# A hybrid encoder trunk: the delta net's first loads, norms and products in a written order on TensorE, VectorE and ScalarE

## The chip, the cores and the metric

One Trainium2 chip, one of its cores. The metric is the device time of one execution in microseconds, the median of several runs. TensorE is PE, VectorE is DVE, ScalarE is ACT, GpSimd is POOL; SP is the engine that issues most DMAs. All data are float32; matrix products run in float32r on a high and a low part of each operand.

## What is computed

A trunk of two layers over 1024 positions of width 1024: a gated delta net, and chunked attention over shared keys and values, each followed by a gated convolution FFN, with RMS norms between. The part that the change touches is the beginning of the delta net:

```python
h = x
xn = rmsnorm(h, a_norm[0])              # x * rsqrt(mean(x*x) + EPS) * g
proj = xn @ a_w_in[0]                   # 1024 x (4096 + 16)
qkv = silu(causal_dwconv(proj[..., :3072], a_conv[0]))   # four taps
z = proj[..., 3072:4096]
b_raw, a_raw = proj[..., 4096:4104], proj[..., 4104:4112]
beta = sigmoid(b_raw)
g = -exp(A_log) * softplus(a_raw + dt_bias)
```

## The kernel before, in words

Activations are kept transposed: 8 tiles of 128 channels, each in two halves `s` of 512 positions. Each is split into a rounded high part `xh[k][s]` (made by ACT, line 1100) and the rest `xl[k][s]` (made by DVE, line 1101); a weight tile of 1024 x 128 is split the same way into `whi` (a cast on ACT, line 103) and `wlo` (POOL, line 105). One product of an output tile is eight units of three PE instructions (`dense`, lines 120 to 122): high by high, high by low, low by high.

The start is `begin_input`. `take_x` issues the load of 128 rows of x (512 KB) on SP's queue. `norm_x` squares and sums a tile on ACT, takes the root, and DVE divides: reciprocal, then one multiply over the whole tile. `turn_x(s)` transposes four such tiles, 128 columns at a time, into a PSUM bank (`pxt`, three banks in turn), from which ACT and DVE make `xh` and `xl` with the norm's gain `g_a`. The first two weight tiles (keys of heads 0 and 1, columns 8 and 9 of 128) are loaded and split at once by `load_w`. Then for each half `s` and each of the two tiles come eight units of products, with one further step of `turn_x` after each unit as long as there is one. `post(s, ps)`, made by `project`, empties the tile's PSUM bank through the four taps of the short convolution (`taps`, DVE) and a silu (tanh on ACT, two operations on POOL). `load_gates`, `project_gates` and `gates` do the 16 columns of beta and the decay.

`colt` (all per-channel constants, 128 x 489, among them `g_a`, the taps `ca`, the FFN's taps) and `rowt` (16 numbers, broadcast to 128 partitions) are loaded at the very top by ACT's own DMA queue; `ca` is halved by DVE soon after.

In the begin PE's order is as written (a manual schedule of PE alone); DVE, ACT and POOL are ordered by the scheduler. Behind the begin a planner, `Flow`, deals out the rest of the delta net by modelled times and writes out the order of PE, DVE and ACT. During the begin it runs in a mode (`auto`) in which `later` calls a step at once.

Of the kernel before, what the change touches and what calls it, by code (L numbers as in the profile page):

```python
# [16 lines left out]
P = 128  # L17
# [11 lines left out]
def trunk_kernel(  # L29
# [22 lines left out]

    ncol = cols.shape[1]
    colt = const.tile([P, ncol], F32, name="colt")
    nc.scalar.dma_start(out=colt, in_=cols)
    o = 0
    def take(n):
        nonlocal o
# [8 lines left out]
    g_b = take(8)  # L67
    g_o = take(1)
    rowt = const.tile([P, 16], F32, name="rowt")
    nc.scalar.dma_start(out=rowt, in_=rows[:, 0:16].broadcast_to([P, 16]))  # L70
    alog = rowt[:, 0:8]
    dtb = rowt[:, 8:16]

# [126 lines left out]
    class Flow(Weave):  # L200
# [4 lines left out]
        def __init__(self):  # L205
            super().__init__()
            self.T, self.free, self.aux = 0.0, dict(D=0.0, A=0.0, G=0.0), deque([[0.0], [0.0]])
            self.time, self.items, self.last, self.stalls = {}, [], 0, []
            self.auto, self.tick, self.slack, self.cur, self.nxt, self.units = True, 0, 0.5, None, deque(), 0
            self.brief, self.early, self.split_at, self.hold = False, 8, 8, None  # L210

        def mark(self, key, t=None):
            super().mark(key)
# [37 lines left out]
            return self.aux[-1]  # L251

        def full(self, rank):
            return rank >= 2 and max(self.free["D"], self.free["A"]) - self.T > 4.0

        def pick(self):
            if self.dense and self.dense[0][0]():
# [252 lines left out]
    with ExitStack() as ph:  # L510
# [11 lines left out]
        nc.vector.tensor_reduce(upper, ident.rearrange("p (b h j) -> p h b j", b=4, h=2)[:, 0], axis=AX.XY, op=ALU.add)  # L522
        early_dp = ExitStack()
        dq = early_dp.enter_context(tc.tile_pool(name="dq", bufs=1, side="right", **SB))

        nc.vector.tensor_scalar(ca, ca, 0.5, None, op0=ALU.mult)

        ba = dp.tile([P, 8, 16], F32, name="ba")

# [539 lines left out]
        def gate_z(hd):  # L1069
            def post(s, ps):  # L1070
                zt = dp.tile([P, HALF], F32, name="zt", tag="zt", bufs=3)
                nc.scalar.copy(zt, ps)
                nc.sync.dma_start(out=d_z[hd][s], in_=zt)
                wv.mark(("z", hd, s), wv.on("A", 0.6) + 3.0)

            return 3072 + hd * P, post
# [6 lines left out]
            x_tiles.append(t_.rearrange("p j t -> p (j t)")[:, 0:SEQ])  # L1083
            nc.sync.dma_start(out=x_tiles[i], in_=x[i * P : (i + 1) * P, :])

        def norm_x(i):
            t_ = x_tiles[i]
            jk = dp.tile([P, 8, P], F32, name="xj", tag="U", bufs=2).rearrange("p c t -> p (c t)")
            r = dp.tile([P, 2], F32, name="rsx", tag="rsx", bufs=4)
            nc.scalar.activation(jk, t_, AF.Square, accum_out=r[:, 0:1])  # L1090
            nc.scalar.activation(r[:, 1:2], r[:, 0:1], AF.Sqrt, scale=1.0 / SEQ, bias=epst)
            nc.vector.reciprocal(r[:, 1:2], r[:, 1:2])
            nc.vector.tensor_scalar(t_, t_, r[:, 1:2], None, op0=ALU.mult)

        def turn_x(s):
            for k in range(KT):
                ps = (pone if k % 3 == 2 else paux).tile([P, HALF], F32, name="pxt", tag="pm" if k % 3 == 2 else "pa")
                for t in range(4):
                    nc.tensor.transpose(ps[:, t * P : (t + 1) * P], x_tiles[4 * s + t][:, k * P : (k + 1) * P], ident)
                nc.scalar.activation(xh[k][s], ps, AF.Copy, scale=g_a[:, k : k + 1])  # L1100
                nc.vector.scalar_tensor_tensor(xl[k][s], ps, g_a[:, k : k + 1], xh[k][s].bitcast(F32), op0=ALU.mult, op1=ALU.subtract)  # L1101
                yield

        def load_gates():
            raw = dp.tile([P, KT, 16], F32, name="raw16", tag="at", bufs=4)
            w16 = dp.tile([P, KT, 32], F32R, name="w16", tag="ke", bufs=4)
            nc.sync.dma_start(out=raw, in_=a_w_in[:, 4096:4112].rearrange("(k p) m -> p k m", p=P))
            nc.scalar.copy(w16[:, :, 0:16], raw)
            nc.gpsimd.tensor_tensor(w16[:, :, 16:32], raw, w16[:, :, 0:16].bitcast(F32), op=ALU.subtract)
            gT = [dq.tile([32, HALF], F32, name="gT", tag="mn", bufs=8) for _ in range(2)]  # L1110
            return w16, gT

        def project_gates(w16, gT, s):
# [49 lines left out]
        def begin_input():  # L1163

            warm = dp.tile([P, 2], F32, name="warm", tag="rsx", bufs=4)
            nc.scalar.activation(warm[:, 0:1], epst, AF.Sqrt)
            for i in range(4):
                take_x(i)
            for i in range(4):
                norm_x(i)  # L1170
            wts = [load_w(a_w_in, m * P) for m in (8, 9)]
            for i in range(4, 8):
                take_x(i)
            for s in range(2):
                if s == 1:
                    for i in range(4, 8):
                        norm_x(i)
                it = turn_x(s)
                for _ in range(3):
                    next(it)  # L1180
                for n, (wt, post) in enumerate(zip(wts, posts)):
                    ps = pacc.tile([P, HALF], F32, name="acc", tag="acc", bufs=3)
                    for i in range(KT):
                        dense(ps, wt, 0, xh, xl, FULL[i : i + 1], s, first=i == 0, last=i == KT - 1)
                        next(it, None)
                        if n == s == 1 and i in (1, 6):
                            next(g_it)
                    post(s, ps)
                    if n == s == 1:
                        break  # L1190
                    if n + s == 0:
                        w16, gT = load_gates()
                    if n + s == 1:
                        project_gates(w16, gT, s)
                    if n == 0 and s == 1:
                        g_it = gates(gT)
            wv.T, wv.free = 0.0, dict.fromkeys(wv.free, 0.0)
            for hd in range(2):
                for s in range(2):
                    wv.mark(("k", hd, s), 3.0 * hd * s)  # L1200
            wv.add(0, "gates", lambda: 0.0, g_it)
# [84 lines left out]
        ORDER = [(w[0], int(w[1])) for w in "k0 k1 k2 k3 q0 q1 k4 q2 q3 k5 v0 v1 k6 v2 v3 k7 q4 q5 q6 q7 v4 v5 v6 v7".split()]  # L1286
        wv = Flow()
        wv.brief, wv.early = True, 5
        with tc.manual_schedule(engines={mybir.EngineType.PE}):
            for w, hd in ORDER:  # L1290
                if w == "k":
                    project(8 + hd, (lambda hd=hd: new_kq(hd), new_u), ("k", hd), {1: d_kq[hd][0]}, 1)
                elif w == "q":
                    project(hd, (lambda hd=hd: kqs[hd, 0][:, 1], new_u), ("q", hd), {1: d_kq[hd][1]}, 1)
                else:
                    project(16 + hd, (new_u, new_u), ("v", hd), d_v[hd])
            for hd in range(6):
                wv.dense.append((lambda: True, lambda: True, dense_tile(*gate_z(hd))))
            wv.dense.append((lambda: True, lambda: True, last_tiles([gate_z(hd) for hd in (6, 7)])))
            xh, xl = act_tiles()  # L1300
            begin_input()
            wv.fetch(0)
            wv.fetch(2)
        wv.auto = False
# [685 lines left out]
    with ExitStack() as ph:  # L1990
# [15 lines left out]
            return lows[i]  # L2006

        wv = Flow()

        def kv_tile(src, c0, g, post):  # L2010

# [556 lines left out]
```

## Time and profile before

| | us |
|---|---|
| median of 3 runs | 2535.78 (2534.97 to 2535.96) |
| profiled execution, its own time | 2536.85 |
| its span, first to last instruction | 2535.1 |
| PE busy | 2494.5 (98%) |
| DVE busy | 1823.7 (72%) |
| ACT busy | 1410.9 (56%) |
| POOL busy | 1479.5 (58%) |
| mean granted clock of PE over the span | 0.997 |

Starts of matmuls are measured; their ends are modelled, so the pace of PE is read from the distance of two starts. The idle time of an engine stands with the group that followed it, with what ended it. A row of the timeline with "x9" is nine instructions, merged; its length is from the first one's start to the last one's end. A plain float32 product stands as two records.

### The profile page before, as it was taken

The numbers are of one execution on the slowest core, as the hardware profiler recorded it, in microseconds if no ns is written. First come the engines' busy times: TensorE is split into PE (matmuls) and PEld (weight loads), VectorE is DVE, ScalarE is ACT, GpSimd is POOL, SyncE is SP. The second block draws the span as 40 slices with busy tenths as digits, with TensorE's granted clock in tenths as the row PEclk, the third lists the DMA queues.
The fourth block names the chain that finished last, engine by engine and source line by source line (L and its number), as shares of the span: only waits on it lengthen the run. The fifth ranks groups of instructions, "written<-read, shape, count | busy, mean of one in ns | idle before, by whom it ended". The sixth has DMA issues, their size and how long they took to land.

```text
span 2535.1 us, 39316 instructions
## 1 busy us (share of the span) xinstructions
PE 2494.5 (98%) x13957; PEld 2076.9 (82%) x13957; DVE 1823.7 (72%) x2962; ACT 1410.9 (56%) x2704; POOL 1479.5 (58%) x1509
## 2 busy tenths in 40 slices
PE   7999999999999999999999999999999999999998
PEld 5878788888878888888788888888877888888877
DVE  5675864555698888888866566666489888888884
ACT  5444555474465555565555555656456565565653
POOL 3655554345448777777625444545443777777770
PEclk9999999999999999999999999999999999999999
DMA  4534435464437677777842112112432577777795
GB/s 128 145 100 119 131 101 174 148 184 145 117 88 153 142 151 154 154 148 159 179 145 63 51 47 62 48 57 77 142 108 88 148 147 145 154 153 153 154 195 186
DMA packets 318853, 325.93 MB, mean 129 GB/s; under 512 B 32832, under 2 KB 243008, under 8 KB 318656
## 3 DMA queue, kind: packets, MB, share of 16 engines
q1 hardware_dynamic: 287840, 220.38, 29.1%
q0 software_dynamic: 25920, 94.38, 20.9%
q10 hardware_dynamic: 4896, 8.65, 1.0%
q8 instruction: 110, 1.80, 0.3%
q14 instruction: 87, 0.71, 0.1%
HBM read 180.68 MB, written 142.67 MB: 128 GB/s over the span
## 4 chain that ended last, share of the span: by engine, by line
PE 82%; DVE 6%; POOL 4%; issue 4%; DMA 2%; ACT 1%; SPq 0%; DVEq 0%; POOLq 0%; ACTq 0%
PE pu L1400 8%; PE pu L1398 8%; PE pu L1399 8%; PE acc L120 7%; PE acc L121 7%; PE acc L122 7%; PE pd L1400 4%; PE pd L1398 4%; PE pd L1399 4%; POOL ul L1364 2%; PE acco L120 2%; PE acco L122 2%; PE acco L121 2%; PE ptp L2210 2%; PE poT L2256 1%
## 5 line engine op out<-in xcount | busy, mean ns | idle before, releaser
L1364 POOL TENSOR_TENSOR ul<-r,uh 128x512 fp32r<-128x512 f32 x270 | 435.8, 1633 | 247.9 <-ACT uh L1386 217.0
L120 PE MATMUL acc<-xh,whi 128*128 128x512 f32 x896 | 375.3, 419 | 0.2 <-ACT xh L1100 0.2
L121 PE MATMUL acc<-xl,whi 128*128 128x512 f32 x896 | 353.3, 394 | 1.0 <-DVE xl L1101 0.6
L105 POOL TENSOR_TENSOR wlo<-wraw,whi 128x256 fp32r<-128x256 f32 (+2 forms) x330 | 236.8, 750 | 198.9 <-ACT whi L103 187.1
L122 PE MATMUL acc<-xh,wlo 128*128 128x512 f32 x896 | 352.5, 393 | 0.0
L1386 ACT CAST uh<-r 128x512 fp32r<-128x512 f32 x290 | 178.1, 623 | 187.8 <-DVE r L1364 160.1
L1398 PE MATMUL pu<-xh,uh 128*128 128x512 f32 x528 | 206.5, 391 | 1.4 <-ACT keep L1527 1.4
L1400 PE MATMUL pu<-xh,ul 128*128 128x512 f32 x528 | 205.9, 390 | 0.6 <-POOL ul L1364 0.6
L1399 PE MATMUL pu<-xl,uh 128*128 128x512 f32 x528 | 205.7, 390 | 0.0
L1748 ACT COPY stage<-pd 128x1024 f32<-128x1024 f32 x180 | 175.6, 1015 | 52.3 <-PE pd L1400 51.8
L122 PEld LDWEIGHTS acc<-xh,wlo 128*128 128x128 f32 x896 | 168.9, 188 | 37.7 <-POOL wlo L105 0.2
L2165 POOL TENSOR_SCALAR sS<-sS,st 128x640 f32<-128x640 f32 (+4 forms) x128 | 86.5, 680 | 181.9 <-DVE st L2163 144.5
L121 PEld LDWEIGHTS acc<-xl,whi 128*128 128x128 f32 x896 | 170.1, 190 | 26.8 <-POOL xl L383 2.4
L120 PEld LDWEIGHTS acc<-xh,whi 128*128 128x128 f32 x896 | 169.8, 190 | 24.9 <-ACT xh L1100 1.0
L1364 POOL TENSOR_TENSOR dl<-a,dh 128x512 fp32r<-128x512 f32 x90 | 152.1, 1690 | 55.2 <-ACT dh L1386 42.3
L1493 DVE SCALAR_TENSOR_TENSOR gate<-gpre,colt,gate 128x1023 f32<-128x1023 f32 (+2 forms) x92 | 174.7, 1899 | 2.5 <-ACT gate L1490 1.8
L1493 DVE SCALAR_TENSOR_TENSOR val<-vpre,colt,val 128x1023 f32<-128x1023 f32 x88 | 146.9, 1669 | 28.7 <-ACT val L1490 28.6
L2155 DVE CUSTOM_DVE_ANT_0 sS<-sc,bt 128x640 f32<-128x640 f32 (+4 forms) x128 | 84.2, 657 | 103.4 <-PE sc L2151 79.5
L1364 DVE TENSOR_TENSOR r<-r,r 128x512 f32<-128x512 f32 x160 | 130.3, 814 | 32.3 <-POOL ul L1364 31.1
L1398 PEld LDWEIGHTS pu<-xh,uh 128*128 128x128 f32 x528 | 99.3, 188 | 22.5 <-ACT keep L1527 2.2
L1400 PEld LDWEIGHTS pu<-xh,ul 128*128 128x128 f32 x528 | 99.3, 188 | 22.0 <-POOL ul L1364 1.3
L1399 PEld LDWEIGHTS pu<-xl,uh 128*128 128x128 f32 x528 | 99.4, 188 | 20.6
(407 smaller groups left out, 7116.7 us busy)
## 6 DMA issues: line engine op xcount, KB each, us to landing
r<-in_f_w_up_dram SPq DMA_DIRECT2D x176, 256.0 KB, 4.3
d_r<-stage POOLq DMA_DIRECT2D x78, 512.0 KB, 7.5
d_c<-stage POOLq DMA_DIRECT2D x70, 512.0 KB, 8.0
a<-in_f_w_down_dram SPq DMA_DIRECT2D x72, 256.0 KB, 2.8
wraw<-in_a_w_in_dram SPq DMA_DIRECT2D x32, 512.0 KB, 4.5
d_e<-stage POOLq DMA_DIRECT2D x32, 512.0 KB, 9.1
wraw<-in_a_w_out_dram SPq DMA_DIRECT2D x16, 512.0 KB, 4.4
d_r<-h ACTq DMA_DIRECT2D x32, 256.0 KB, 3.2
```

What stands on the lines that cost most here:

```text
L105: nc.gpsimd.tensor_tensor(lo[:, c], raw[:, c], hi[:, c].bitcast(F32), op=ALU.subtract)
L120: mm(ps, hi[:, kw, wcol : wcol + P], rh[k][s], start=st, stop=False)
L121: mm(ps, hi[:, kw, wcol : wcol + P], rl[k][s], start=False, stop=False)
L122: mm(ps, lo[:, kw, wcol : wcol + P], rh[k][s], start=False, stop=sp)
L1364: tt = lambda eng, o, a, b, op: eng.tensor_tensor(o, a, b, op=op)
L1386: copy(hi, src)
L1398: mm(ps, w[0][:, cw], x[0], start=first, stop=False, skip_group_check=True)
L1399: mm(ps, w[0][:, cw], x[1], start=False, stop=False, skip_group_check=True)
L1400: mm(ps, w[1][:, cw], x[0], start=False, stop=last, skip_group_check=True)
L1493: nc.vector.scalar_tensor_tensor(t_[:, a:c1], p_[:, a - step : c1 - step], w[:, 2 - step : 3 - step], t_[:, a:c1], op0=ALU.mult, op1=ALU.add)
L1748: nc.scalar.copy(t_, ps)
L2165: nc.gpsimd.tensor_scalar(S, S, st[:, 3:4], 1.0, op0=ALU.mult, op1=ALU.mult)
```

## The change

The two loads of `colt` and `rowt` leave ACT's queue and the top of the kernel: `colt` goes on SP's queue behind x tiles 0 to 3 and ahead of the two weight tiles, `rowt` behind x tiles 4 to 7. PE begins with 18 products of the identity with itself into a PSUM tile that nobody reads (`idle`); further ones stand behind each x tile's transposes (6, 4, 4, 2). The first three `pxt` banks are filled tile by tile as the x tiles come, instead of bank by bank; the fourth x tile is multiplied in two halves. The first weight tile is cast in two halves, the second only after the second unit of products. The norms of tiles 4 to 7, the halving of `ca`, the first tile's taps and silu and the loads of the gates get written places; `later` collects steps for `go_on` to place. The transposes of the second half come ahead of the gates' products of the first half. The whole begin is now a manual schedule of PE, DVE and ACT. The planner's limits `far` (4.0, before a constant) and `slack` (0.5) have names now and their old values.

```diff
-    nc.scalar.dma_start(out=colt, in_=cols)
...
-    nc.scalar.dma_start(out=rowt, in_=rows[:, 0:16].broadcast_to([P, 16]))
...
-        nc.vector.tensor_scalar(ca, ca, 0.5, None, op0=ALU.mult)
...
-        def norm_x(i):
+        def norm_x(i, n=1):
...
-            nc.vector.tensor_scalar(t_, t_, r[:, 1:2], None, op0=ALU.mult)
+            for c in range(n):
+                c = slice(c * SEQ // n, (c + 1) * SEQ // n)
+                nc.vector.tensor_scalar(t_[:, c], t_[:, c], r[:, 1:2], None, op0=ALU.mult)
...
+        def own_x(k, s, ps):
+            nc.scalar.activation(xh[k][s], ps, AF.Copy, scale=g_a[:, k : k + 1])
+            nc.vector.scalar_tensor_tensor(xl[k][s], ps, g_a[:, k : k + 1], xh[k][s].bitcast(F32), op0=ALU.mult, op1=ALU.subtract)
...
             for i in range(4):
                 take_x(i)
-            for i in range(4):
-                norm_x(i)
-            wts = [load_w(a_w_in, m * P) for m in (8, 9)]
+            nc.sync.dma_start(out=colt, in_=cols)
+            raws = [raw_tile(m * P) for m in (8, 9)]
             for i in range(4, 8):
                 take_x(i)
...
+            nc.sync.dma_start(out=rowt, in_=rows[:, 0:16].broadcast_to([P, 16]))
+            idle = pchain.tile([P, P], F32, name="idle", tag="pc0", bufs=1)
+
+            def keep_busy(n):
+                for _ in range(n):
+                    mm(idle, ident, ident, start=True, stop=True)
+
+            keep_busy(18)
+            pxt = [(pone if k == 2 else paux).tile([P, HALF], F32, name="pxt", tag="pm" if k == 2 else "pa") for k in range(3)]
+            for t in range(4):
+                norm_x(t, 2 if t == 3 else 1)
+                for k in range(3):
+                    nc.tensor.transpose(pxt[k][:, t * P : (t + 1) * P], x_tiles[t][:, k * P : (k + 1) * P], ident)
+                keep_busy((6, 4, 4, 2)[t])
+            hi = wp.tile([P, KT, P], F32R, name="whi", tag="whi")
+            lo = wp.tile([P, KT, P], F32R, name="wlo", tag="wlo")
+            for c in (slice(0, 4), slice(4, 8)):
+                nc.scalar.copy(hi[:, c], raws[0][:, c])
+            for c in range(0, 8, 2):
+                nc.gpsimd.tensor_tensor(lo[:, c : c + 2], raws[0][:, c : c + 2], hi[:, c : c + 2].bitcast(F32), op=ALU.subtract)
+            for k in range(3):
+                own_x(k, 0, pxt[k])
...
+            it = turn_x(0, 3)
+            more = lambda: next(it, None)
+            after = {i: [more] for i in range(KT)}
+            after[1].append(lambda: wts.append(split_w(raws[1], [P, KT, P])))
+            after[3].append(lambda: nc.vector.tensor_scalar(ca, ca, 0.5, None, op0=ALU.mult))
+            after[4].append(lambda: norm_x(4))
+            after[6].append(lambda: norm_x(5))
+            pending = deque()
+            wv.later = lambda t, f: pending.append(f)
+            go_on = lambda: pending.popleft()()
+            first = tile_of(0, 0, after)
+            gT = []
+            second = tile_of(1, 0, {0: [lambda: norm_x(6)], 1: [lambda: norm_x(7)], 2: [lambda: posts[0](0, first), lambda: gT.extend(load_gates())], 3: [go_on]})
+            it = turn_x(1)
+            for _ in range(3):
+                more()
+            go_on()
+            posts[1](0, second)
+            go_on()
+            w16, gT = gT
+            project_gates(w16, gT, 0)
+            after = {i: [more] for i in range(KT)}
+            after[1].append(go_on)
+            posts[0](1, tile_of(0, 1, after))
+            del wv.later
+            go_on()
+            project_gates(w16, gT, 1)
+            g_it = gates(gT)
+            posts[1](1, tile_of(1, 1, {1: [lambda: next(g_it)], 6: [lambda: next(g_it)]}))
```

How the instructions stand now, at three places. Names: `pxt` bank of transposes, `xt` x tile, `acc` output tile, `accg` the gates' products, `xj` scratch of the squares, `rsx` the sums; a number after `xh` or `xl` is its half and a running number. First PE at its very start, before:

```order
L1099 MATMUL pxt<-ident,xt 128x128 x12
L120 MATMUL acc<-xh_0_238,whi 128x512
L121 MATMUL acc<-xl_0_239,whi 128x512
L122 MATMUL acc<-xh_0_238,wlo 128x512
L1099 MATMUL pxt<-ident,xt 128x128 x4
L120 MATMUL acc<-xh_0_242,whi 128x512
L121 MATMUL acc<-xl_0_243,whi 128x512
L122 MATMUL acc<-xh_0_242,wlo 128x512
```

and now:

```order
L1179 MATMUL idle<-ident 128x128 x18
L1186 MATMUL pxt<-ident,xt 128x128 x3
L1179 MATMUL idle<-ident 128x128 x6
L1186 MATMUL pxt<-ident,xt 128x128 x3
L1179 MATMUL idle<-ident 128x128 x4
L1186 MATMUL pxt<-ident,xt 128x128 x3
L1179 MATMUL idle<-ident 128x128 x4
L1186 MATMUL pxt<-ident,xt 128x128 x3
L1179 MATMUL idle<-ident 128x128 x2
L118 MATMUL acc<-xh_0_233,whi 128x512
L119 MATMUL acc<-xl_0_234,whi 128x512
L120 MATMUL acc<-xh_0_233,wlo 128x512
```

All twelve transposes of the first three banks stood together; now they come by x tile, with the products of the identity between.

PE at the end of the second tile's first half, before:

```order
L120 MATMUL acc<-xh_0_266,whi 128x512
L121 MATMUL acc<-xl_0_267,whi 128x512
L122 MATMUL acc<-xh_0_266,wlo 128x512
L1116 MATMUL accg<-xh_0_238,w_422 32x512
L1117 MATMUL accg<-xl_0_239,w_422 16x512
...
L1116 MATMUL accg<-xh_0_266,w_422 32x512
L1117 MATMUL accg<-xl_0_267,w_422 16x512
L1099 MATMUL pxt<-ident,xt 128x128 x12
L120 MATMUL acc<-xh_1_240,whi 128x512
L121 MATMUL acc<-xl_1_241,whi 128x512
L122 MATMUL acc<-xh_1_240,wlo 128x512
L1099 MATMUL pxt<-ident,xt 128x128 x4
```

and now:

```order
L118 MATMUL acc<-xh_0_261,whi 128x512
L119 MATMUL acc<-xl_0_262,whi 128x512
L120 MATMUL acc<-xh_0_261,wlo 128x512
L1101 MATMUL pxt<-ident,xt 128x128 x12
L1117 MATMUL accg<-xh_0_233,w_486 32x512
L1118 MATMUL accg<-xl_0_234,w_486 16x512
...
L1117 MATMUL accg<-xh_0_261,w_486 32x512
L1118 MATMUL accg<-xl_0_262,w_486 16x512
L118 MATMUL acc<-xh_1_235,whi 128x512
L119 MATMUL acc<-xl_1_236,whi 128x512
L120 MATMUL acc<-xh_1_235,wlo 128x512
L1101 MATMUL pxt<-ident,xt 128x128 x4
```

The twelve transposes of the second half moved ahead of the sixteen gate products.

ACT at its start, before:

```order
L1090 ACTIVATE xj,rsx<-xt 128x1024 x2
L1091 ACTIVATE rsx<-rsx,epst 128x1 x2
L1090 ACTIVATE xj,rsx<-xt 128x1024 x2
L1091 ACTIVATE rsx<-rsx,epst 128x1 x2
L103 CAST whi<-wraw 128x1024 x2
L1100 ACTIVATE xh_0_238<-pxt,colt 128x512
L1100 ACTIVATE xh_0_242<-pxt,colt 128x512
L1100 ACTIVATE xh_0_246<-pxt,colt 128x512
L1090 ACTIVATE xj,rsx<-xt 128x1024
L1100 ACTIVATE xh_0_250<-pxt,colt 128x512
L1108 CAST w_422<-raw_421 128x8x16
```

and now:

```order
L1086 ACTIVATE xj,rsx<-xt 128x1024
L1087 ACTIVATE rsx<-rsx,epst 128x1
L1086 ACTIVATE xj,rsx<-xt 128x1024
L1087 ACTIVATE rsx<-rsx,epst 128x1
L1191 CAST whi<-wraw 128x512 x2
L1094 ACTIVATE xh_0_233<-pxt,colt 128x512
L1094 ACTIVATE xh_0_237<-pxt,colt 128x512
L1094 ACTIVATE xh_0_241<-pxt,colt 128x512
L1094 ACTIVATE xh_0_245<-pxt,colt 128x512
L1094 ACTIVATE xh_0_249<-pxt,colt 128x512
L101 CAST whi<-wraw 128x1024
L1094 ACTIVATE xh_0_253<-pxt,colt 128x512
```

Each root follows its square; one weight tile's cast, in halves, stands ahead of the first `xh` in place of two, and the square of x tile 4 is no longer between the third and the fourth `xh`.

## Rows read from the trace of the kernel before

**Rows 1.** The page's chain that ended last: share of the span by engine.

```profile
PE 82%; DVE 6%; POOL 4%; issue 4%; DMA 2%; ACT 1%; SPq 0%; DVEq 0%; POOLq 0%; ACTq 0%
```

**Rows 2.** Busy time by stretch: engines, then granted clock, DMA share, GB/s.

```profile
0.00:16.00 16.00, 3.32 (x12) 2.33 (x12) 4.08 (x12) 9.47 (x18) 4.21 (x16) 1.00 0.86 281
```

**Rows 3.** Timeline, first issues: start us, length us, engine, line, operation, tiles, count.

```profile
0.80 0.41 ACTq L55 DMA_DIRECT2D colt<-in_cols_dram  x1
...
0.80 2.01 SPq L1084 DMA_DIRECT2D xt<-in_x_dram  x4
...
1.19 0.29 POOL masks.py:199 TENSOR_SCALAR_AFFINE_SELECT ident<-ident 128x128 f32<-128x128 f32 x1
...
1.25 0.45 ACTq L70 DMA_DIRECT2D rowt<-in_rows_dram  x1
...
2.85 2.52 SPq L111 DMA_DIRECT2D wraw<-in_a_w_in_dram  x2
```

**Rows 4.** DMA packets and ACT's queue (q10), 5.5 to 7.5; packets 8 to 10.

```profile
DMA packets 157, 0.27 MB, mean 134 GB/s; under 512 B 93, under 2 KB 93, under 8 KB 157
...
q10 hardware_dynamic: 78, 0.00, 2.0%
...
DMA packets 319, 0.81 MB, mean 403 GB/s; under 512 B 25, under 2 KB 136, under 8 KB 319
```

**Rows 5.** Timeline of ACT at the start; in brackets idle time and releaser.

```profile
10.85 1.06 ACT L1090 ACTIVATE xj<-xt 128x1024 f32<-128x1024 f32 x1 [0.19 <-DMA xt<-in_x_dram]
...
12.63 1.05 ACT L103 CAST whi<-wraw 128x1024 fp32r<-128x1024 f32 x1 [0.26 <-DMA wraw<-in_a_w_in_dram]
...
15.35 1.84 ACT L1100 ACTIVATE xh<-pxt,colt 128x512 fp32r<-128x512 f32 x3
...
25.35 1.06 ACT L1090 ACTIVATE xj<-xt 128x1024 f32<-128x1024 f32 x1
...
26.53 0.29 ACT L1091 ACTIVATE rsx<-rsx,epst 128x1 f32<-128x1 f32 x1
```

**Rows 6.** Timeline of DVE at the start.

```profile
9.55 0.75 DVE L1093 TENSOR_SCALAR xt<-xt,rsx 128x1024 f32<-128x1024 f32 x1
```

**Rows 7.** Timeline of PE, its first transposes and products.

```profile
14.08 2.18 PE L1099 MATMUL pxt<-ident,xt 128*128 128x128 f32 x9 [0.38 <-DVE xt L1093]
...
16.08 0.80 PE L120 MATMUL acc<-xh,whi 128*128 128x512 f32 x1
...
16.87 0.80 PE L121 MATMUL acc<-xl,whi 128*128 128x512 f32 x1
...
19.17 0.63 PE L121 MATMUL acc<-xl,whi 128*128 128x512 f32 x1
...
19.60 0.53 PE L122 MATMUL acc<-xh,wlo 128*128 128x512 f32 x1
...
20.64 0.39 PE L121 MATMUL acc<-xl,whi 128*128 128x512 f32 x1
...
20.86 0.39 PE L122 MATMUL acc<-xh,wlo 128*128 128x512 f32 x1
```

**Rows 8.** Timeline of PE: second tile, gates, second half's transposes, its gates.

```profile
26.69 0.39 PE L120 MATMUL acc<-xh,whi 128*128 128x512 f32 x1
...
32.16 0.39 PE L1116 MATMUL accg<-xh,w 128*32 128x512 f32 x1
...
35.86 1.47 PE L1099 MATMUL pxt<-ident,xt 128*128 128x128 f32 x12
...
38.29 0.50 PE L121 MATMUL acc<-xl,whi 128*128 128x512 f32 x1 [0.29 <-DVE xl L1101]
...
46.14 0.39 PE L1116 MATMUL accg<-xh,w 128*32 128x512 f32 x1
```

**Rows 9.** Timeline of PE: four plain float32 products of 128x128.

```profile
75.64 1.05 PE L716 MATMUL pg<-kq 128*128 128x128 f32 x8
```

**Rows 10.** Waits of PE: engine, line, who was waited for, us, times, longest.

```profile
PE po L989 <- DVE mn L728: 3.4, 1, 3.4
```

More of the change, by code (lines that the diff above doesn't have):

```diff
@@ L209, in __init__ @@
             self.auto, self.tick, self.slack, self.cur, self.nxt, self.units = True, 0, 0.5, None, deque(), 0
-            self.brief, self.early, self.split_at, self.hold = False, 8, 8, None
+            self.brief, self.early, self.split_at, self.hold, self.far = False, 8, 8, None, 4.0
         def mark(self, key, t=None):
@@ L253, in full @@
         def full(self, rank):
-            return rank >= 2 and max(self.free["D"], self.free["A"]) - self.T > 4.0
+            return rank >= 2 and max(self.free["D"], self.free["A"]) - self.T > self.far
         def pick(self):
@@ L1092, in norm_x, with turn_x @@
             nc.vector.reciprocal(r[:, 1:2], r[:, 1:2])
-            nc.vector.tensor_scalar(t_, t_, r[:, 1:2], None, op0=ALU.mult)
-        def turn_x(s):
-            for k in range(KT):
+            for c in range(n):
[4 more added lines that the diff above has]
+            nc.vector.scalar_tensor_tensor(xl[k][s], ps, g_a[:, k : k + 1], xh[k][s].bitcast(F32), op0=ALU.mult, op1=ALU.subtract)
+        def turn_x(s, k0=0):
+            for k in range(k0, KT):
                 ps = (pone if k % 3 == 2 else paux).tile([P, HALF], F32, name="pxt", tag="pm" if k % 3 == 2 else "pa")
@@ L1099, in turn_x @@
                     nc.tensor.transpose(ps[:, t * P : (t + 1) * P], x_tiles[4 * s + t][:, k * P : (k + 1) * P], ident)
-                nc.scalar.activation(xh[k][s], ps, AF.Copy, scale=g_a[:, k : k + 1])
-                nc.vector.scalar_tensor_tensor(xl[k][s], ps, g_a[:, k : k + 1], xh[k][s].bitcast(F32), op0=ALU.mult, op1=ALU.subtract)
+                own_x(k, s, ps)
                 yield
@@ L1168, in begin_input @@
                 take_x(i)
-            for i in range(4):
-                norm_x(i)
-            wts = [load_w(a_w_in, m * P) for m in (8, 9)]
+            nc.sync.dma_start(out=colt, in_=cols)
+            raws = [raw_tile(m * P) for m in (8, 9)]
             for i in range(4, 8):
                 take_x(i)
[L1174 to L1196, printed above, removed]
@@ new lines, in begin_input @@
+            hi = wp.tile([P, KT, P], F32R, name="whi", tag="whi")
[6 more added lines that the diff above has]
+                own_x(k, 0, pxt[k])
+            wts = [(hi, lo)]
@@ new lines, in tile_of @@
+            def tile_of(n, s, after):
+                ps = pacc.tile([P, HALF], F32, name="acc", tag="acc", bufs=3)
+                for i in range(KT):
+                    dense(ps, wts[n], 0, xh, xl, FULL[i : i + 1], s, first=i == 0, last=i == KT - 1)
+                    for f in after.get(i, ()):
+                        f()
+                return ps
+            it = turn_x(0, 3)
+            more = lambda: next(it, None)
+            after = {i: [more] for i in range(KT)}
+            after[1].append(lambda: wts.append(split_w(raws[1], [P, KT, P])))
@@ L1288, in trunk_kernel @@
         wv.brief, wv.early = True, 5
-        with tc.manual_schedule(engines={mybir.EngineType.PE}):
[L1290 to L1301, printed above, removed]
+        wv.slack = 0.5
+        wv.far = 4.0
+        for w, hd in ORDER:
+            if w == "k":
+                project(8 + hd, (lambda hd=hd: new_kq(hd), new_u), ("k", hd), {1: d_kq[hd][0]}, 1)
+            elif w == "q":
+                project(hd, (lambda hd=hd: kqs[hd, 0][:, 1], new_u), ("q", hd), {1: d_kq[hd][1]}, 1)
+            else:
+                project(16 + hd, (new_u, new_u), ("v", hd), d_v[hd])
+        for hd in range(6):
+            wv.dense.append((lambda: True, lambda: True, dense_tile(*gate_z(hd))))
+        wv.dense.append((lambda: True, lambda: True, last_tiles([gate_z(hd) for hd in (6, 7)])))
+        xh, xl = act_tiles()
+        with tc.manual_schedule(engines={mybir.EngineType.PE, mybir.EngineType.DVE, mybir.EngineType.Activation}):
+            begin_input()
+        with tc.manual_schedule(engines={mybir.EngineType.PE}):
             wv.fetch(0)
@@ L2008, in trunk_kernel @@
         wv = Flow()
+        wv.slack = 0.5
+        wv.far = 4.0
         def kv_tile(src, c0, g, post):
```

## The prediction

> **What bounds the kernel now.** The chain that ended last is TensorE for 82% [rows 1], so what counts is when PE gets work, and only at the places where it lacks it. The largest is the start: of the first 16 us PE is busy for 3.32 [rows 2]. I read the start in four steps. First the queues: SP issues the x tiles from 0.80, while ACT issues colt and rowt on its own queue from 0.80 and 1.25; the two weight tiles follow on SP at 2.85 [rows 3]. Then what the transfers do: from 5.5 to 7.5 us the DMA engines move 0.27 MB in 157 packets, 78 of them the 64-byte packets of ACT's queue (they fall one for one with SP's); from 8 to 10, with SP's queue alone, they move 0.81 MB [rows 4]. Then ACT: the fourth x tile is there at 10.85, the first weight tile at 12.63, and the first xh is made only at 15.35, behind both weight casts [rows 5]. Last PE: the first real product starts at 16.08; products still start 0.43 us apart at 19.17 and 19.60 (512 columns at 1.2 GHz), and 0.22 apart from 20.64 (2.4 GHz) [rows 7]. The granted-clock column reads 1.00 through this stretch [rows 2], so here the distances of the starts have to be read, not the column. Before that rise PE had done a few transposes and waited between them.
>
> **The change, part by part** (times from the span's start; "now" means after the change).
>
> *Loads.* rowt goes behind the eight x tiles, colt behind the first four. In 5.5 to 7.5 the lost traffic is 0.81 - 0.27 = 0.54 MB, at 0.403 MB per us 1.3 us [rows 4]. colt's 0.25 MB (128 x 489 float32) is 0.6 us at that rate and no longer stands among x0 to x3. So x3 lands at 10.85 - 1.3 - 0.6 = 8.9. The first weight tile still has colt ahead of it and gains only the 1.3: 12.63 - 1.3 = 11.3 [rows 5]. SP's queue gains two issues of about 0.5 us; x0 to x3 are ahead of both, and rowt's first reader is the gates' arithmetic some 25 us later, so I cost those at nothing.
>
> For the price of such packets there is a rule to weigh. The Trainium skill, "DMA: Bandwidth & Descriptors", section "Why small descriptors are slow (HBM only)", charges a packet with a fixed overhead of about three bus cycles; by that 128 packets of 64 bytes would be nearly free and moving rowt would give nothing. The rows on the two queues speak against it [rows 4]; the sum by it is that of the first rival, worked out there.
>
> *Fourth tile in halves, ACT and DVE in program order.* Square and root of x3 follow its landing by about 1.4, the multiply of a whole tile takes 0.75 [rows 6], of a half about 0.4; k0 to k2 lie in the first half. PE could transpose at about 11.1. That is before the weight tile is in, so the halving itself is worth nothing more unless loads come faster. What sets xh0 is ACT's order: now the first weight's cast alone stands ahead of it, in two halves, 1.05 together, 11.3 to 12.3 (before, a second cast at 14.40 was in the way, too). From xh0's start to the first product it was 16.08 - 15.35 = 0.73 [rows 5, 7], so 13.0.
>
> *Dummy products.* 34 plain float32 products of 128x128, 32 of them ahead of x3's transposes. No row shows them on an idle PE; the nearest are the four products per head behind pg, which stand as 8 records and take 1.05 us, 0.22 each once pipelined at 2.4 GHz [rows 9]; at 1.2 GHz 0.43. Bounds: all at the upper level, and PE is ready for each tile as it comes, at no cost; all at the lower, and, begun when the identity is built (1.5, [rows 3]), x3's transposes end at 1.5 + 32 x 0.43 + 12 x 0.22 = 17.9. A transpose at the lower level is from the nine that take 2.18 us [rows 7]. I take a mix nearer to the upper bound, since before the change sparser work had brought PE to the upper level by 20.64: about the first dozen slow and the rest fast, each group behind its tile. That ends x3's transposes at 12.5, 0.2 behind the cast. First product then 13.2, against 16.08. The bounds for this are 13.0 and 18.7.
>
> *Clock.* Before, from 16.08 to about 20.0, PE did six products and four transposes in 3.9 us. At 0.23 and 0.11 each they are 1.8 us; the wait for the first xl stays (0.80 between the first two products where 0.23 would do, about 0.55). So 2.35 and 1.5 us saved, if the dummies have raised the level.
>
> *First tile.* Now unit 0 ends at 13.2 + 1.25 = 14.45, then seven units of three products (0.69) and five groups of four transposes (0.44) are 7.0, and the halving of the taps ahead of the last xl some 0.2: 21.65. ACT and DVE no longer do the norms of x4 to x7 in between. Before, the second tile's first product was at 26.69 [rows 8]. Gain 5.0. The second tile is the same 24 products.
>
> *Between the halves.* The second tile ends at 27.1 and the transposes of x4 to x7 come next. ACT makes their norms behind xh7: 20.3 plus four times 1.36 (square at 25.35, root at 26.53, and 0.18 to the next [rows 5]) is 25.75, reciprocal and multiply to about 26.9: covered with only 0.2 to spare. Each further 0.2 us that ACT is late then shows on PE. After the transposes come the 16 gate products (3.7 us, 32.16 to 35.86 [rows 8]), which now hide the first three xh and xl of the second half. Before, transposes ended at 35.86 + 1.47 = 37.33, and from there to the gates of the second half at 46.14 is 8.81 us for 8 x 0.69 + 5 x 0.44 = 7.7 of work: 1.1 of waits, the largest before the second product at 38.29 [rows 8]. I take 1.0 of it as gone. What is queued behind the moved steps: the first tile's taps on DVE now stand ahead of xl of the second half (three of 0.75), and they end at about 29.4, with the first need at 32. The second tile's taps end near 35, just ahead of the fourth xl; no margin, no cost.
>
> *Gates' chain.* ACT now copies the second half's gates after a tanh that waits for taps, and PE splits its eight small transposes around one product of the next tile. By the same durations that copy ends at about 45.8 and PE wants it at 45.9. Zero, with 0.3 either way.
>
> *Everything later.* The order on all five engines is the same from there to the end, and the planner's two numbers have their old values. Zero.
>
> **Sum:** 5.0 + 1.0 = 6.0 us. Profiled execution: 2536.85 (span 2535.1) becomes 2530.85 (2529.1). It lies 1.07 above the median of the runs, 2535.78, so the forecast against the median is 2529.8. A measurement of this kernel can tell about 0.2%, that is 5.07 us: faster means below 2530.7, slower above 2540.9. The forecast lies just 0.9 beyond that line.
>
> **Rivals.**
> *1. The weight tile comes no earlier,* because rowt's packets only happened to lie in a slow stretch. Then the cast starts at 12.63, the first product at 14.4, 1.2 later than forecast: gain 4.8, 2531.0. For it: one stretch only was seen. Against: the packets alternate one for one and the rate is back where they have ended [rows 4]. 14%. By the section of the Trainium skill named above ("DMA: Bandwidth & Descriptors") it would go this way.
> *2. The gain is partly given back.* Later stalls exist whose size could change: in the delta net PE waits once 3.4 us for DVE [rows 10]. Half of such a stall, or ACT late by a us before the transposes of x4 to x7, leaves 2 to 4.5: about 2532.5. Against: same order, all engines shifted together. 16%.
> *3. The dummies don't keep the level up.* PE is idle for about half a us before the first product, and then products run 0.43 apart again: 1.5 back, 2531.3. 7%.
> *4. Slower: the dummies stand in front.* If all of them run at 1.2 GHz, x3's transposes end at 17.9 and the first product is at 18.7, 5.5 later than forecast; with the level still low behind them another 1.5. The first tile ends at 28.7 instead of 26.69, 1.0 comes back between the halves: 1.0 slower, 2536.8. It decides once x3's transposes end later than about 16.9. Against: in the trace before, far sparser work raised the level by 20 us. 4%.
> *5. More:* that stall shrinks, or the loads come faster without a second queue: gain 7 to 8.5, 2528. 7%.
>
> **How the numbers follow.** The forecast itself (gain 5.1 to 6.9) has 52%. Faster by over 0.2%: forecast and rival 5, 0.60 with a little of the others. Within: rivals 1, 2, 3 and most of 4, 0.36. Slower by over 0.2%: 0.04, should rival 4 and a given-back gain meet. The range takes in the forecast, rivals 1 and 3 and most of 2, and about half of 5; rival 4 and the far ends of 2 and 5 stay out: 2527.3 to 2533.5.
>
> **What would show it.** x3's square begins at about 8.9 and the first weight cast at 11.3; if the cast stays at 12.6, rival 1. Dummy starts 0.43 apart at first and 0.22 later, all over before 13; the first product near 13.2, the third product 0.23 after the second. The second tile starts near 21.7, the transposes of x4 to x7 near 27.1 with no wait ahead, the second gates near 40.1. If that is 6 earlier and the end is not, rival 2, and the wait of rows 10 is the first place to look. I am wrong if the first product is later than 14.5 or the gain at the second gates is under 5.

## The result, and the profile after

| | before | after |
|---|---|---|
| median, runs taken side by side | 2535.3 (2532.69 to 2537.62, 22 runs) | 2537.9 (2533.04 to 2543.05, 22 runs) |
| profiled execution, its own time | 2536.85 | 2534.87 |
| its span | 2535.1 | 2533.2 |

The ratio after to before is 1.0013 [1.0007, 1.0019]: 3.3 us more, between 1.8 and 4.8 (2.6 by the medians). That is clear of zero but within the bound of 0.2%; against the forecast, 2529.8, it is 8.1 us too long, outside the range and on its other side. The profiled execution of after is one of its quicker ones, so the two spans read alone would say 1.9 faster. The places in the traces have to say what happened.

The page's chain and the first 16 us of after, which answer to [rows 1, 2]:

```profile
PE 86%; DVE 5%; POOL 3%; issue 3%; DMA 1%; ACT 1%; SPq 0%; DVEq 0%; POOLq 0%; ACTq 0%
```

```profile
0.00:16.00 16.00, 14.08 (x90) 13.35 (x91) 6.33 (x15) 10.29 (x20) 4.75 (x16) 1.00 0.93 320
```

PE's 14.08 against 3.32 is mostly products of the identity. What counts is when real work starts. ACT of after (the columns of [rows 5]):

```profile
8.54 1.04 ACT L1086 ACTIVATE xj<-xt 128x1024 f32<-128x1024 f32 x1
...
10.84 1.14 ACT L1191 CAST whi<-wraw 128x512 fp32r<-128x512 f32 x2 [0.83 <-DMA wraw<-in_a_w_in_dram]
...
12.89 1.84 ACT L1094 ACTIVATE xh<-pxt,colt 128x512 fp32r<-128x512 f32 x3 [0.91 <-PE pxt L1186]
```

PE of after, against [rows 7 to 9]:

```profile
1.52 7.12 PE L1179 MATMUL idle<-ident 128*128 128x128 f32 x36 [1.52 <-POOL epst L77]
8.47 0.49 PE L1186 MATMUL pxt<-ident,xt 128*128 128x128 f32 x3
...
12.91 0.61 PE L1179 MATMUL idle<-ident 128*128 128x128 f32 x4
13.63 0.50 PE L118 MATMUL acc<-xh,whi 128*128 128x512 f32 x1
...
22.28 0.40 PE L118 MATMUL acc<-xh,whi 128*128 128x512 f32 x1
...
27.77 1.47 PE L1101 MATMUL pxt<-ident,xt 128*128 128x128 f32 x12
...
40.74 0.40 PE L1117 MATMUL accg<-xh,w 128*32 128x512 f32 x1
...
69.99 1.05 PE L712 MATMUL pg<-kq 128*128 128x128 f32 x8
```

The begin does nearly what was forecast. The first product is at 13.63 instead of 16.08, the second gates at 40.74 instead of 46.14 (5.4 earlier), `pg` at 69.99 instead of 75.64 (5.65 earlier). Matching the matmuls of both traces one by one (times of before), after stays 4.8 to 7.7 ahead from 38 us to the norm at 668, where it is 7.0 ahead, and is 2.1 ahead at 672. Of the 7.0, 2.7 came near 308, where the granted clock falls in before's trace and not in after's. So 4.9 are lost in one place, in the norm ahead of the first FFN. First SP's queue there, before:

```profile
648.16 1.43 SPq L1444 DMA_DIRECT2D r<-in_f_w_up_dram  x2
...
651.34 18.96 SPq L1444 DMA_DIRECT2D r<-in_f_w_up_dram  x10
```

and after, with its queue's waits (who was waited for: us, times, longest):

```profile
640.96 0.50 SPq L1485 DMA_DIRECT2D r<-in_f_w_up_dram  x1
...
654.10 0.37 SPq L1485 DMA_DIRECT2D r<-in_f_w_up_dram  x1
...
659.60 7.16 SPq L1485 DMA_DIRECT2D r<-in_f_w_up_dram  x10
```

```profile
SPq L1485 <- DVE run L359: 17.6, 2, 12.6
```

where in before SP's one wait for DVE in this stretch is

```profile
SPq L1444 <- DVE rsn L377: 0.5, 1, 0.5
```

`r` are the FFN's up-weight tiles. Before, the first three issues came within 3.2 us; after, the second and the third wait for DVE's sum of squares (`run`, in `norm_steps`), 17.6 us together. Then ACT and PE, before:

```profile
666.57 0.61 ACT L1386 CAST uh<-r 128x512 fp32r<-128x512 f32 x1
...
668.60 0.27 ACT L376 ACTIVATE rsn<-pss,epst 128x8 f32<-128x8 f32 x1 [0.51 <-PE pss L374]
```

```profile
669.20 1.11 PE L387 MATMUL psb<-ident,rsn 128*128 128x128 f32 x8
```

and after:

```profile
662.68 0.62 ACT L1427 CAST uh<-r 128x512 fp32r<-128x512 f32 x1 [3.08 <-DMA r<-in_f_w_up_dram]
664.39 0.62 ACT L1427 CAST dh<-r 128x512 fp32r<-128x512 f32 x1 [1.09 <-DMA r<-in_f_w_up_dram]
664.91 0.26 ACT L374 ACTIVATE rsn<-pss,epst 128x8 f32<-128x8 f32 x1
```

```profile
665.47 1.38 PE L385 MATMUL psb<-ident,rsn 128*128 128x128 f32 x8 [3.11 <-DVE rsn L375]
```

ACT's order is the same in both. But now the cast `uh` waits 3.08 us for its late load, the norm's root (`rsn`) stands behind it, and PE, which needs the root for `psb`, waits 3.11 us. Behind that wait the granted clock of after falls to half for 3.4 us (0.51 in this row of busy time by stretch), which gives away another 1.6 against before:

```profile
666.30:669.70 3.40, 3.40 (x11) 2.72 (x11) 2.79 (x5) 1.24 (x2) 0.73 (x2) 0.51 1.21 293
```

Why should those loads wait for DVE? The instruction order on all five engines is identical there. What is not identical are addresses: of all SBUF buffers of the two programs, only those of three rings lie elsewhere. The rings of the pool `dp` lie in SBUF in the order in which their tags are first used. The three stand next to each other: `zt` (three buffers: `th`, `sq` of the norm, and others), `at` (with `raw16`) and `ke` (with `w16`). Before, the first silu (`th`) came ahead of `load_gates`; in the change the silu is collected by `later` and comes behind it. From the two programs, in bytes within a partition:

| ring | before | after |
|---|---|---|
| zt | 149696 to 155839 | 166080 to 172223 |
| at | 155840 to 164031 | 149696 to 157887 |
| ke | 164032 to 172223 | 157888 to 166079 |
| the FFN's first three `r` tiles (2048 each) | 161760, 165856, 167904 | the same |

After, the second and the third `r` tile lie on `zt`, and `zt` is the ring in which the norm's squares are still being added up when these loads are due.

### The profile page after: what moved, and what is told of

Same layout as the page of the kernel before. It is cut to its first block, busy times and chain, and to the rows that moved or that the text cites. A ratio compares the mean times of both kernels' runs of the same rounds, so it can differ in the third digit from the quotient of the medians.

```text
span 2533.2 us, 39460 instructions
## 1 busy us (share of the span) xinstructions
PE 2499.8 (99%) x14025; PEld 2084.9 (82%) x14025; DVE 1823.6 (72%) x2963; ACT 1409.8 (56%) x2705; POOL 1476.6 (58%) x1509
## 4 chain that ended last, share of the span: by engine, by line
PE 86%; DVE 5%; POOL 3%; issue 3%; DMA 1%; ACT 1%; SPq 0%; DVEq 0%; POOLq 0%; ACTq 0%
PE pu L1441 9%; PE pu L1439 9%; PE pu L1440 9%; PE acc L118 7%; PE acc L119 7%; PE acc L120 7%; PE pd L1439 4%; PE pd L1441 4%; PE pd L1440 4%; PE acco L118 2%; PE acco L120 2%; PE acco L119 2%; PE ptp L2253 2%; POOL ul L1405 2%; PE poT L2299 1%
## 5 line engine op out<-in xcount | busy, mean ns | idle before, releaser
L103 POOL TENSOR_TENSOR wlo<-wraw,whi 128x256 fp32r<-128x256 f32 (+1 forms) x326 | 233.7, 748 | 186.3 <-ACT whi L101 174.5
```

The source lines that it names most:

```text
L103: nc.gpsimd.tensor_tensor(lo[:, c], raw[:, c], hi[:, c].bitcast(F32), op=ALU.subtract)
```

## The experiments

All start from the change or from the kernel before, and each was timed in five rounds side by side with the kernel before, whose medians in the three sets were 2535.71, 2535.3 and 2535.22. Theory P says that the addresses of these rings took the gain.

**e1_place: the change, with the addresses of before.** Reserving `zt` ahead of `at` changes no instruction.

```diff
         def load_gates():
+            for _ in range(3):
+                dp.tile([P, HALF], F32, name="held", tag="zt", bufs=3)
             raw = dp.tile([P, KT, 16], F32, name="raw16", tag="at", bufs=4)
```

> The changed kernel, its instructions in the same order on all engines, with three unused buffers of the ring zt reserved ahead of the gates' buffers, so that the rings zt, at and ke lie at the addresses they have in the kernel before. Theory P (placement: in the changed kernel the first up-weight tiles r12 and r21 of the FFN lie on the squares of the last norm and wait for DVE): their loads wait for no DVE, the wait of PE for rsn near 665 us is gone, and the gain of the begin stays: 5 us below the kernel before, about 2530. Rival T (the FFN's loads are late because everything is 5 to 7 us earlier, whatever the addresses) and rival C (clock): as the changed kernel, 2536 to 2539.

**e2_moved: the kernel before, with the addresses of after.** The begin is the old one.

```diff
+                for tag in ("at", "ke"):
+                    for _ in range(4 * (s == 0)):
+                        dp.tile([P, HALF], F32, name="held", tag=tag, bufs=4)
```

> The kernel before, order unchanged, with the rings at and ke reserved ahead of zt, so that the three rings lie at the addresses of the changed kernel. Theory P: begin as before, but the loads of r12 and r21 wait for DVE, PE waits some 3 us near 672 and may drop its clock there: 4 to 8 us slower than the kernel before, 2539 to 2543. Rivals T and C: as the kernel before, 2535.

**e3_after:** the change itself, once more beside them.

> The changed kernel as it is, for a second trace beside the others on one chip. Both theories: 2 to 4 us slower than the kernel before. Theory P: again a wait of PE for DVE's rsn near 665 and SP's second up-weight load held for more than 10 us by DVE's running sum. Open is how often the granted clock falls there.

Measured:

| | median | ratio to before |
|---|---|---|
| e1_place | 2531.95 (2529.75 to 2536.15) | 0.9983 [0.9975, 0.9992] |
| e2_moved | 2541.5 (2539.66 to 2544.63) | 1.0025 [1.0014, 1.0035] |
| e3_after | 2538.48 (2535.44 to 2540.26) | 1.0011 [1.0002, 1.0020] |

The addresses alone cost the old begin 5.8 us by the medians, and giving them back saves the new one 6.5. In e1_place PE does not wait:

```profile
664.98 1.11 PE L385 MATMUL psb<-ident,rsn 128*128 128x128 f32 x8
```

and in e2_moved, whose begin is that of before, the wait of after is there (waits of PE):

```profile
PE psb L387 <- DVE rsn L377: 3.1, 1, 3.1
```

So P holds in both directions; T and C expected no change from either edit. e3_after's trace has the wait again (PE 2.99 us at 670.86). Of the 5.8, the two traces before and e2_moved show 5.2 where they part: 3.6 up to the end of the wait, 1.6 more while the clock is low.

How often does the clock fall there? In all four traces where PE waits here behind a held load (after, e2_moved, e3_after, e8_between) it does; in before and e1_place, without that wait, it doesn't. But in the times that fall is not all. The mean granted clock of the runs is 0.9965 in the 33 runs of the change, 0.9968 in e2_moved, 0.9979 in e1_place and 0.9983 in the 75 runs of before. If PE works throughout, 0.0018 of 2535 us is 4.6 us between the change and before (an estimate from these), of which the fall behind the wait is 1.6. The rest would be lost at other falls; why they come more often in the change, no run shows.

**e8_between: zt between the other two rings,** at 157888 to 164031. Is it that one overlap, or any placement other than the old one?

```diff
             raw = dp.tile([P, KT, 16], F32, name="raw16", tag="at", bufs=4)
+            for _ in range(3):
+                dp.tile([P, HALF], F32, name="held", tag="zt", bufs=3)
             w16 = dp.tile([P, KT, 32], F32R, name="w16", tag="ke", bufs=4)
```

> The change with the ring of the norms' squares (tag zt) reserved between the two rings at and ke instead of behind them: zt at 157888, where it lies neither in before nor after; at lies as in after, ke as in before. The FFN's first two up-weight tiles then overlap ke, not zt. Theory (it is this one overlap that makes their loads wait for DVE): no such wait, no stall at 665, time as e1_place, 2531 to 2533. Rival (any placement other than that of before costs, by the at ring or by other overlaps): 2535 or more.

Measured: 2540.79 (2537.59 to 2543.65), ratio 1.0024 [1.0014, 1.0035], the rival's number. But the expectation had overlooked an address: the first `r` tile lies at 161760, and that is where `zt` now lies. The trace shows the same mechanism one load earlier (SP's issues and its waits, ACT, PE):

```profile
663.95 8.51 SPq L1487 DMA_DIRECT2D r<-in_f_w_up_dram  x11
```

```profile
SPq L1487 <- DVE nacc L364: 19.4, 1, 19.4
```

```profile
669.91 0.62 ACT L1429 CAST uh<-r 128x512 fp32r<-128x512 f32 x1 [6.72 <-DMA r<-in_f_w_up_dram]
```

```profile
667.64 0.80 PE L1441 MATMUL pu<-xh,uh 128*128 128x512 f32 x1 [6.21 <-POOL uh L1429]
```

```profile
664.00:674.20 10.20, 6.43 (x17) 4.75 (x17) 0.00 (x0) 1.24 (x2) 6.18 (x6) 0.50 0.95 245
```

With the very first load held, all of them queue behind it on SP; PE waits 6.2 instead of 3.1, and the granted clock is 0.50 for 10.2 us. What e8_between was meant to tell apart it doesn't: a placement that is new and free of this overlap was not tried. But the wait follows the overlap, tile for tile, in five kernels: none in before and e1_place, the second and third load in after and e2_moved, the first in e8_between.

**e4_nodummy: e1_place without the identity products.**

```diff
-                for _ in range(n):
+                for _ in range(0):
                     mm(idle, ident, ident, start=True, stop=True)
```

> e1_place with none of the 34 products of the identity (left out; they feed nothing). If they are worth the clock, as forecast: the first product starts earlier (x tiles no longer wait for PE: near 12.6 in place of 13.6), but products start 0.43 us apart until about 17 or later, so 1 to 2 us slower than e1_place. If the clock rises as soon without them: 1 us faster than e1_place.

Measured: 2531.7 (2529.82 to 2533.27), 0.9985 [0.9977, 0.9994], no different from e1_place. The trace shows two effects. Without them the x tiles' transposes start 0.7 to 1.1 earlier and the first product is at 12.73 instead of 13.00. Then products run at the lower level (starts 0.41 to 0.59 apart) until about 16:

```profile
15.24 0.78 PE L118 MATMUL acc<-xh,whi 128*128 128x512 f32 x1
15.82 0.57 PE L119 MATMUL acc<-xl,whi 128*128 128x512 f32 x1
16.23 0.40 PE L120 MATMUL acc<-xh,wlo 128*128 128x512 f32 x1
```

The second gates come at 41.05 instead of 40.08: from the first product on 1.24 is lost, and 0.27 was won ahead of it. The 34 products are worth 1.0 net in this pair of traces, less than these runs tell in the time.

**e5_loads: e1_place with both small loads back on ACT's queue at the top.**

```diff
     colt = const.tile([P, ncol], F32, name="colt")
+    nc.scalar.dma_start(out=colt, in_=cols)
...
     rowt = const.tile([P, 16], F32, name="rowt")
+    nc.scalar.dma_start(out=rowt, in_=rows[:, 0:16].broadcast_to([P, 16]))
...
-            nc.sync.dma_start(out=colt, in_=cols)
...
-            nc.sync.dma_start(out=rowt, in_=rows[:, 0:16].broadcast_to([P, 16]))
```

> e1_place with the loads of colt and rowt back at the very top on ACT's own queue; nothing else differs. Theory (the load order carries part of the begin's gain): by the kernel before, x tile 3 lands near 10.85 and the first weight tile near 12.63, where e1_place had 8.70 and 11.00; the first product comes near 14.6 instead of 13.0, the end 1.6 later: about 2533.5, ratio to before near 0.9990. Rival (the new order of casts and transposes does it all, the queue nothing): first product within 0.3 of 13.0 and the time within 0.5 of e1_place.

Measured: 2535.26 (2529.02 to 2539.57), 0.9998 [0.9989, 1.0007]: 3.3 above e1_place by the medians instead of 1.6, but the intervals reach down to that, and in the traces the second gates come 1.57 later (41.65). The DMA view from 5.5 to 7.5 is that of [rows 4] again:

```profile
DMA packets 166, 0.28 MB, mean 138 GB/s; under 512 B 100, under 2 KB 100, under 8 KB 166
...
q10 hardware_dynamic: 84, 0.01, 2.1%
```

where e1_place has

```profile
DMA packets 222, 0.83 MB, mean 417 GB/s; under 512 B 18, under 2 KB 19, under 8 KB 222
```

The first cast and the first product of e5_loads:

```profile
12.74 1.14 ACT L1193 CAST whi<-wraw 128x512 fp32r<-128x512 f32 x2 [0.28 <-DMA wraw<-in_a_w_in_dram]
```

```profile
14.52 0.50 PE L120 MATMUL acc<-xh,whi 128*128 128x512 f32 x1 [0.17 <-ACT xh L1096]
```

The cast is 1.74 later than e1_place's 11.00, the product 1.52 later than its 13.00. colt's bytes stand ahead of the weight tile in both kernels, so those 1.74 are the price of ACT's queue running beside SP's. It is rowt's packets that cost. From 3 to 4 us of before, colt's packets (1956 bytes) alternate with SP's just so, and the DMA engines move 0.39 MB in 1 us:

```profile
DMA packets 127, 0.39 MB, mean 388 GB/s; under 512 B 0, under 2 KB 62, under 8 KB 127
...
q10 hardware_dynamic: 62, 0.12, 34.1%
```

By the rule of the Trainium skill ("DMA: Bandwidth & Descriptors", section "Why small descriptors are slow (HBM only)") the packets of rowt should have been nearly free. Their own records agree: the 84 packets of q10 took 2.1% of the DMA engines' time. But the traffic beside them falls to a third, which that rule does not give; what holds up SP's packets between them no run shows.

**e6_gates: e1_place with the gates' products ahead of the second half's transposes again.**

```diff
-            it = turn_x(1)
-            for _ in range(3):
-                more()
             go_on()
-            posts[1](0, second)
-            go_on()
             w16, gT = gT
             project_gates(w16, gT, 0)
+            it = turn_x(1)
+            for _ in range(3):
+                more()
+            posts[1](0, second)
+            go_on()
```

> e1_place with the sixteen gate products of the first half ahead of the twelve transposes of the second half again, as before the change. Theory (the forecast's term between the halves): PE waits about 1.0 more between the last transposes and the second half's products, and the second gates come 1.0 later. Rival A: the gates' place is worth nothing (0 to 0.3), because the second half's xh and xl were covered either way by the taps and casts that now have written places. Rival B: worth more, 1.5 to 2, because ACT's copy of the gates now stands ahead of the second half's xh. In the time 1 us is at the edge of what five rounds tell, so the place of the second gates in the trace decides.

Measured: 2534.2 (2531.0 to 2536.65), 0.9995 [0.9986, 1.0003]. The second gates are at 42.10, against 40.08 in e1_place; 0.2 of the 2.0 was there at the first product (13.18). PE waits again for `xl`:

```profile
37.66 0.50 PE L119 MATMUL acc<-xl,whi 128*128 128x512 f32 x1 [0.53 <-DVE xl L1095]
...
42.10 0.39 PE L1119 MATMUL accg<-xh,w 128*32 128x512 f32 x1
```

That is 1.8, rival B, which bears out the term between the halves in kind. It is more than the 1.0 forecast: ACT's copy of the gates (31.46) now stands ahead of the three `xh` (31.94), which costs about 1.0 up to the second product, and at 37.66 a further 0.7 goes, where ACT's tanh of the second tile (37.04) stands ahead of an `xh`.

**e7_order: a better begin.** The two traces suggest it: PE behind its own identity products (`xh` waits 0.91 for `pxt`), and the cast waiting 0.83 for a weight tile with colt ahead of it.

```diff
-            nc.sync.dma_start(out=colt, in_=cols)
-            raws = [raw_tile(m * P) for m in (8, 9)]
+            raws = [raw_tile(8 * P)]
+            nc.sync.dma_start(out=colt, in_=cols)
+            raws.append(raw_tile(9 * P))
...
-            keep_busy(18)
+            keep_busy(12)
...
-                keep_busy((6, 4, 4, 2)[t])
+                keep_busy((2, 2, 2, 0)[t])
```

> e1_place with the first weight tile's load ahead of colt, and 18 identity products in place of 34: 12 in front and 2 behind each of the first three x tiles' transposes, none behind the fourth's. Theory (PE stands behind its own identity products by about 0.7 per x tile, and the cast waits 0.84 for the weight tile): x tiles' transposes start within 0.2 of their multiplies, the first cast starts near 10.3 instead of 11.0, the first product near 12.2 instead of 13.0, and the level is still raised ahead of it; end 0.8 earlier than e1_place, about 2531.1. Rival A: fewer identity products leave the level low until the first products, which then come 0.43 apart, and the gain is lost again. Rival B: colt, now later, holds the first xh; first product at 12.8 or later.

**e9_none: e7_order without its 18 identity products.**

```diff
-            keep_busy(12)
+            keep_busy(0)
...
-                keep_busy((2, 2, 2, 0)[t])
+                keep_busy(0)
```

> e7_order without its 18 identity products; nothing else differs. In e4_nodummy taking out all 34 cost 0.8 behind the first products (the upper level came at 16.2 instead of 6.2), and gave back 0.7 to 1.1 at the x tiles' transposes. In e7_order PE is no longer behind its own identity products. Theory (the level is worth what the forecast's clock term says, once the identity products are out of the way): first product at 12.1 as in e7_order, products 0.43 apart for about 3 us behind it, the second tile 0.8 to 1.5 later than in e7_order; the time 0.8 to 1.5 above 2530.3, about 2531.4. Rival (they are worth nothing, since xh and xl set the pace of the first products): second tile within 0.3 of e7_order.

Measured: e7_order 2530.3 (2527.36 to 2533.72), 0.9980 [0.9971, 0.9989], ahead of before and of the change. e9_none 2532.4 (2526.93 to 2535.08), 0.9988 [0.9979, 0.9997]. In e7_order the first product and the second half's transposes are at

```profile
12.14 0.50 PE L118 MATMUL acc<-xh,whi 128*128 128x512 f32 x1 [0.56 <-ACT xh L1094]
...
26.23 1.47 PE L1101 MATMUL pxt<-ident,xt 128*128 128x128 f32 x12
```

and in e9_none

```profile
12.47 0.79 PE L118 MATMUL acc<-xh,whi 128*128 128x512 f32 x1 [0.38 <-ACT xh L1094]
...
27.98 1.25 PE L1101 MATMUL pxt<-ident,xt 128*128 128x128 f32 x10
```

Every step of e7_order's expectation came: first product 0.86 before e1_place's, second gates 0.88 before. Of the 0.86, 0.66 is the first cast, which no longer waits for a weight tile behind colt (10.34 against 11.00); 0.2 is left for PE, no longer late behind identity products. Without the 18 the second gates are 1.75 later (40.95 against 39.20). Of that, 0.33 is there at the first product, because the cast came 0.35 later behind its load (10.69); from there on 1.42 is lost, the theory's side. The medians of e9_none and e7_order differ by 2.1, more than the 0.8 to 1.5 expected, and those of e7_order and e1_place by 1.65; the intervals separate neither. The traces separate e7_order and e1_place in the begin alone: at 600 us 0.5 of the 0.88 is left.

## Why the prediction was wrong

**The step that failed** is "Everything later": "The order on all five engines is the same from there to the end ... Zero." The order is the same. The addresses are not, and where rings of one pool give way to tiles of the next, an address becomes a wait of a DMA for an engine. It took 6.5 by the medians of e3_after and e1_place, more than the 5.4 that the begin gained in the trace of after. Rival 2, "the gain is partly given back", had the sign of this but the wrong place and size: it looked to the stall of [rows 10], which is unchanged in after at 3.4, and allowed 4 at most. Rival 4, the only one on the slow side, rested on identity products that stayed slow; in after their records start 0.21 apart until 7.44 and 0.11 from there.

The other steps, each at its place:

- *Loads.* Square of x3 forecast at 8.9, came at 8.54; first cast at 11.3, came at 10.84. Right, if a little small: e5_loads gives 1.74 at the cast (forecast 1.3) and 1.5 at the first product; rival 1 is refuted.
- *Fourth tile in halves.* Costed at nothing; no run tried it alone.
- *Identity products.* The last x tile's transposes were to end at 12.5; they started at 12.58, because PE stood behind 14 slow products in front and six between the first two tiles. So `xh` waited 0.91 for PE and not for the cast, and the first product was at 13.63 instead of 13.2. This differs from run to run: with the same products from 1.52 on, the records go from 0.21 to 0.11 apart at 7.44 in after, 6.16 in e1_place, 5.10 in e8_between and 4.89 in e3_after. In e3_after, the same kernel, PE is in time and waits 0.43 for `xh`, and the second gates come 0.85 earlier than in after:

```profile
12.76 0.50 PE L118 MATMUL acc<-xh,whi 128*128 128x512 f32 x1 [0.43 <-ACT xh L1094]
...
39.89 0.40 PE L1117 MATMUL accg<-xh,w 128*32 128x512 f32 x1
```

- *Clock.* Forecast 1.5 saved by the level; from the first product on e7_order against e9_none gives 1.4, e1_place against e4_nodummy 1.2. Right.
- *First tile and between the halves.* Second tile forecast at 21.65, came at 22.28 in after (21.43 in e3_after): gain 4.4 instead of 5.0. From there to the second gates 1.0 more, as forecast.
- *Gates' chain.* Zero within 0.3; from the second gates to `pg` the gain went from 5.4 to 5.65. Right.

The begin therefore gained 5.4 of the 6.0 in after, and 6.1 to 6.4 in the three other traces with the same begin (second gates at 40.08, 39.89 and 39.78, forecast 40.1): from the first product to the second gates all four take 27.1, and only the first product moves. e1_place, the change as the prediction imagined it, ran at 2531.95: inside the range, 2.15 above the forecast, 3.8 below the kernel before [2.0, 6.3].

What could have shown it beforehand: not the instruction order, whose rows name tiles and no addresses, but the addresses of the rings that the change uses first in another order, laid beside those of the pool that follows. That was not looked at.

## What to carry to other kernels

A step that is moved also moves the first use of its buffers, and with it the place of every ring that is laid out afterwards: compare addresses, and who waits for whom, before costing the rest of a program at zero. When a gain at one end does not reach the other, match the two traces instruction by instruction and look for the place where the distance jumps; a wait on a DMA queue that is in one trace alone is the thing to explain. Work that only keeps an engine busy has to end before the real work is ready, or it is the new wait.

## What was not expected of the hardware

The runs of one kernel spread over 8 us, and the mean granted clock goes with it: in 75 runs of the kernel before, the median is 2532.3 at 1.000 (5 runs), 2533.9 at 0.999 (26), 2535.8 at 0.998 (32) and 2537.4 at 0.997 (11), with one run at 0.996. The traces show where: the granted clock falls to half for some us at places that differ from run to run (before: 306.6 and 1873.3; e1_place: 152.9 and 303.1; e5_loads: none ahead of 2524). At or just ahead of each of these places PE has a wait of 1.2 to 3.4 us, and in e5_loads those near 153 and 304 (2.3 and 3.4 us) pass without a fall. So a stall can cost more than its own length: 3.1 us in the norm and 1.6 behind it. That is also why the profiled execution of after, low for 6.8 us ahead of its last stretch, could end ahead of that of before, low for 10.2, while the medians say the opposite.
